# A row softmax on one core: pieces of columns for the first and the last tile, and a quarter of the scaling on another engine

## The chip, the cores and the metric

The kernel runs on one core of a Trainium2 chip. The time is device microseconds (us) of that core. The engines that matter here are VectorE (DVE in the profile), ScalarE (ACT), SyncE (SP, which does nothing but wait and issue transfers) and the core's 16 DMA engines, which move data between the chip's main memory and the on-chip memory of 128 partitions.

## The reference

A softmax over the last axis of a float32 array of 16 x 256 rows with 32768 columns, after a division by a temperature that is 1.0:

```python
scaled = logits / temperature
scaled = scaled - scaled.max(axis=-1, keepdims=True)
exp_scaled = np.exp(scaled)
return (exp_scaled / exp_scaled.sum(axis=-1, keepdims=True)).astype(np.float32)
```

Input and output are 536.87 MB each.

## The kernel before

Each row of 32768 columns is laid over two neighbouring partitions, as two halves of 16384 columns (64 KB each). A tile is 64 rows, so 128 partitions by 16384 columns, 8.4 MB; there are 64 tiles, numbered 0 to 63. The on-chip memory holds three such tiles, in three buffers `b` = 0, 1, 2 of one tensor `xs`; tile g lives in buffer g mod 3.

A tile is loaded and stored by two DMAs of 4.2 MB. One carries the even partitions, one the odd ones (h = 0, 1, lines 79 to 89). Each partition's 64 KB are contiguous in main memory. Semaphores `ld[b][h]` and `st[b][h]` count the landings.

A tile is computed in K = 4 pieces of 4096 columns, by two engines that signal each other:

- DVE waits for both halves of the load (line 105), then reduces each piece to the negated maximum of each partition (line 107).
- ACT takes each piece as its maximum arrives and replaces it with exp(x - maximum of the piece), summing as it goes (line 153).
- After the fourth exponential (line 116) DVE exchanges maxima and sums between neighbouring partitions (line 118), takes the row's maximum (line 122); ACT computes the correction of each piece, exp(piece's maximum - row's maximum), into `ee` (line 163); DVE sums the corrected sums (line 126) and takes the reciprocal (line 137).
- DVE multiplies each of the four pieces in place with its correction and the reciprocal (line 141). The last of them raises the semaphore `sc` (line 144).
- `stores` waits for `sc` and issues the two DMAs out (lines 171 to 174).

The order is written out by hand in four instruction streams. SP issues the loads of tiles 0, 1, 2 at once (183 to 185), then in a loop of 20 turns over three buffers waits for each half's store and issues the load of the next tile in its place (186 to 190), and in the end the load of tile 63 (191 to 193). DVE and ACT run the same tiles in the same order: 20 turns of three tiles, then tiles 60 to 63 written out (196 to 211). ACT issues the stores of tiles 0 to 60 itself, behind each tile's last small exponential (207, 211). SP issues the stores of tiles 61, 62 and 63, behind its last load (214 and 215), and waits for all stores (216 to 218).

## Time and profile before

| | us |
|---|---|
| median of 3 timed runs | 2526.8 |
| the runs | 2759.95, 2513.87, 2526.8 |
| profiled execution, its own time | 2492.2 |
| its span | 2490.4 |
| DVE busy | 1756.9 (71%) |
| ACT busy | 1017.9 (41%) |
| one reduce of a piece (128x4096), DVE, line 107 | 4.41 |
| one exponential of a piece, ACT, line 153 | 3.71, and 0.19 for reading the sum |
| one scaling of a piece, DVE, line 141 | 2.41 |
| first reduce begins / first store is issued | 23.4 / 55.5 |
| last reduce of tile 63 begins / its store is issued | 2449.2 / 2468.2 |

The profile is of one execution on the chip. Its page gives the busy time of each engine, the share of time in which the DMA engines were busy and the rate that they reached in 40 slices of the span, and groups of instructions by the line of the kernel. Queries of the same trace give waits, a timeline and the rates in chosen stretches. The share of the DMA engines can come out above 1 in a short stretch, since a packet is counted where it starts; stretches of a few us are read with that in mind. The profiled execution is somewhat shorter than the timed ones, so its rows are summed against its own time.

### The profile page before, as it was taken

What the parts mean: (1) busy time and instruction counts of PE and PEld (TensorE: products, weight loads), DVE (VectorE), ACT (ScalarE), POOL (GpSimd) and SP (SyncE); (2) the same over time, 40 slices, a digit from 0 to 9 for tenths busy, and PEclk for the clock granted to TensorE, in tenths of its full rate; (3) what the DMA queues carried; (4) which work ended last, traced back from release to release, by engine and by line L of the source; (5) the groups of instructions that cost most, each with busy time, mean ns of one, the idle gap of its engine ahead of it and who ended that gap; (6) DMA issues with size and microseconds to landing.
All of it is one profiled execution on the core that took longest, in us unless ns stands there. A gap on an engine that the chain in (4) does not pass through costs nothing.

```text
span 2490.4 us, 2598 instructions
## 1 busy us (share of the span) xinstructions
DVE 1756.9 (71%) x896; ACT 1017.9 (41%) x596; POOL 0.2 (0%) x4
## 2 busy tenths in 40 slices
DVE  5876676777767767777677776777767767777675
ACT  3444342534434334344353443434434335244342
POOL 0000000000000000000000000000000000000000
DMA  9999999999999999999999999999999999999999
GB/s 415 427 438 436 426 429 434 435 435 431 434 436 437 433 432 435 437 435 429 435 436 437 429 435 435 435 435 432 435 435 436 429 436 434 437 434 432 434 398 389
DMA packets 20482, 1073.77 MB, mean 431 GB/s; under 512 B 4096, under 2 KB 4096, under 8 KB 4096
## 3 DMA queue, kind: packets, MB, share of 16 engines
q1 hardware_dynamic: 10720, 562.05, 52.3%
q10 hardware_dynamic: 9760, 511.71, 47.4%
q14 instruction: 2, 0.02, 0.0%
HBM read 536.87 MB, written 536.87 MB: 431 GB/s over the span
## 4 chain that ended last, share of the span: by engine, by line
DMA 53%; DVE 24%; another core or an unknown queue 14%; ACT 4%; issue 3%; SPq 1%; DVEq 0%; ACTq 0%
DMA out_dram<-xs 29%; DMA xs<-in_logits_dram 24%; DVE t L107 17%; DVE xs L141 7%; ACT xs L153 4%; SPq L86 1%; ACT ee L163 0%; DVE t L118 0%; DVE row L137 0%; DVE row L122 0%; DVE junk L126 0%; ACTq L89 0%; DVEq L196 0%; DVEq L117 0%
## 5 line engine op out<-in xcount | busy, mean ns | idle before, releaser
L153 ACT ACTIVATE xs<-xs,t 128x4096 f32<-128x4096 f32 x256 | 949.2, 3708 | 1184.0 <-DVE t L107 1184.0
L107 DVE TENSOR_REDUCE t<-xs 128x1 f32<-128x4096 f32 x256 | 1113.4, 4411 | 425.0 <-DMA xs<-in_logits_dram 425.0
L141 DVE TENSOR_SCALAR xs<-xs,ee,row 128x4096 f32<-128x4096 f32 x256 | 600.4, 2408 | 2.3
L118 DVE LOAD_MASK_SELECT t<-t x64 | 0.9, 14 | 255.2 <-ACT xs L153 255.2
L153 ACT ACT_TABLE_LOAD x20 | 25.7, 1283 | 219.8 <-issue 218.8
L153 ACT ACTIVATION_READ_ACCUMULATOR xs<-xs,t 128x1 f32 x256 | 47.7, 186 | 0.0
L163 ACT ACTIVATE ee<-t,row 128x8 f32<-128x8 f32 x64 | 19.2, 301 | 36.7 <-DVE row L122 36.7
L126 DVE CUSTOM_DVE_ANT_1 junk<-ee,t 128x8 f32<-128x8 f32 x64 | 10.7, 167 | 23.5 <-ACT ee L163 23.5
L137 DVE RECIPROCAL row<-row 128x1 f32<-128x1 f32 x64 | 10.5, 164 | 2.2
L122 DVE TENSOR_REDUCE row<-t 128x1 f32<-128x8 f32 x64 | 10.3, 161 | 2.4 <-DVE t L118 0.3
L118 DVE STREAM_SHUFFLE t<-t 128x8 f32<-128x8 f32 x64 | 10.6, 165 | 0.6
L126 DVE DVE_READ_ACCUMULATOR2_ANT row<- 128x1 f32 x64 | 5.3, 82 | 0.0
L235 POOL MEMSET const-bfloat16-1.0<- 128x1 bf16 x1 | 0.1, 101 | 0.0
L235 POOL MEMSET const-uint8-127<- 128x1 uint8 x1 | 0.1, 101 | 0.0
L235 POOL MEMSET const-float32-0.0<- 128x1 f32 x1 | 0.1, 98 | 0.2 <-issue 0.2
L235 POOL MEMSET const-float32-1.0<- 128x1 f32 x1 | 0.1, 98 | 0.0
## 6 DMA issues: line engine op xcount, KB each, us to landing
xs<-in_logits_dram SPq DMA_DIRECT2D x128, 28.9
out_dram<-xs ACTq DMA_DIRECT2D x122, 39.8
out_dram<-xs SPq DMA_DIRECT2D x6, 24.2
```

The costliest lines, as they stand in the source:

```text
L86: sp.dma_start(out=sbuf(b, h), in_=dram(x, g, h)).then_inc(ld[b][h], 16)
L107: m = dve.tensor_reduce(out=t[:, k : k + 1], in_=self.piece(k), axis=X_, op=A.max, negate=True)
L118: dve.stream_shuffle(out=t[:, 2 * K : 4 * K], in_=t[:, 0 : 2 * K], mask=swap).then_inc(site(tag, "sh"), 1)
L122: dve.tensor_reduce(out=r[:, 0:1], in_=tv[:, :, 0, :], axis=XY, op=A.min).then_inc(site(tag, "mx"), 1)
L126: dve.tensor_tensor_reduce(out=j[:, 0 : 2 * K].rearrange("p (a k) -> p a k", a=2), in0=e[:, 0 : 2 * K].rearrange("p (a k) -> p a k", a=2), ...
L137: dve.reciprocal(out=r[:, 2:3], in_=r[:, 1:2]).then_inc(site(tag, "rc"), 1)
L141: s = dve.tensor_scalar(out=xs, in0=xs, scalar1=e[:, k : k + 1], scalar2=r[:, 2:3], op0=A.mult, op1=A.mult)
L153: a = act.activation(out=xs, in_=xs, func=Exp, bias=t[:, k : k + 1], scale=inv_t, accum_out=t[:, K + k : K + k + 1],)
L163: act.activation(out=e[:, 0 : 2 * K].rearrange("p (a k) -> p a k", a=2), in_=tv[:, :, 0, :], func=Exp, bias=r[:, 0:1], scale=-1.0,).then_i ...
L235: nc = _bacc.Bacc("TRN2", target_bir_lowering=False, num_devices=1)
```

## The change

Three edits:

- Tile 0 is loaded by four DMAs, one for each piece of 4096 columns over all 128 partitions (16 KB of each partition), with a semaphore each, `pieces[k]`. DVE waits for piece k just ahead of its reduce. To this end tile 0 is taken out of the loops of DVE and ACT: `first()` is tile 0, the loops hold tiles 1 to 60, and tiles 61 to 63 are written out behind them. SP's loops are unchanged.
- In every tile DVE scales three pieces. It also multiplies the last piece's correction with the reciprocal into one factor per partition, `r[:, 3:4]`, and ACT multiplies the last piece with that factor, by an activation with the function Copy and the factor as its scale. Each scaling raises a semaphore of its own, `sc` with k. `stores` waits for those of pieces 2 and 3 (DVE works in order, so piece 2 stands for 0 and 1).
- Tile 63 is stored by four DMAs, one for each piece of columns, each issued by SP when that piece is scaled.

```diff
+    def columns(b, k):
+        return X[:, b * _W + k * _STEP : b * _W + (k + 1) * _STEP]
+
+    def dram_columns(t, g, k):
+        return t[bass.ds(g * P, P), k * _STEP : (k + 1) * _STEP]
...
-            for h in range(_PARTS):
-                dve.wait_ge(ld[self.b][h], self.landed)
             for k in range(K):
+                for sem, value in self.landed if k == 0 or self.fine else []:
+                    dve.wait_ge(sem[k] if self.fine else sem, value)
...
-            for k in range(K):
+            dve.tensor_tensor(
+                out=r[:, 3:4], in0=e[:, K - 1 : K], in1=r[:, 2:3], op=A.mult
+            ).then_inc(site(tag, "f"), 1)
+            for k in range(K - 1):
                 xs = self.piece(k)
-                s = dve.tensor_scalar(
+                dve.tensor_scalar(
                     out=xs, in0=xs, scalar1=e[:, k : k + 1], scalar2=r[:, 2:3], op0=A.mult, op1=A.mult
-                )
-            s.then_inc(site(tag, "sc"), 1)
+                ).then_inc(site(tag, "sc", k), 1)
...
+            xs = self.piece(K - 1)
+            act.wait_ge(site(tag, "f"), n)
+            act.activation(out=xs, in_=xs, func=Copy, scale=r[:, 3:4]).then_inc(
+                site(tag, "sc", K - 1), 1
+            )

         def stores(self, q, g):
-            q.wait_ge(site(self.tag, "sc"), self.n)
+            for k in range(K - 2, K):
+                q.wait_ge(site(self.tag, "sc", k), self.n)
             for h in range(_PARTS):
                 store(q, g, self.b, h)
...
+        def stores_in_columns(self, q, g, sem):
+            for k in range(K):
+                q.wait_ge(site(self.tag, "sc", k), self.n)
+                q.dma_start(out=dram_columns(o, g, k), in_=columns(self.b, k)).then_inc(sem, 16)
...
+    pieces = [nc.alloc_semaphore(f"piece{k}") for k in range(K)]
+    for k in range(K):
+        sp.dma_start(out=columns(0, k), in_=dram_columns(x, 0, k)).then_inc(pieces[k], 16)
+    for b in range(1, _BUFS):
         for h in range(_PARTS):
             load(b, b, h)
...
+    first().vector()
     with dve.Fori(1, turns + 1) as i:
-        for b in range(_BUFS):
-            turn(b, i).vector()
-    for g in range(G - 4, G):
+        for q in range(_BUFS):
+            turn(q, i).vector()
+    for g in range(G - 3, G):
         last(g).vector()
...
+    first().scalar()
+    first().stores(act, 0)
     with act.Fori(1, turns + 1) as i:
-        for b in range(_BUFS):
-            tile_ = turn(b, i)
+        for q in range(_BUFS):
+            tile_ = turn(q, i)
             tile_.scalar()
-            tile_.stores(act, i * _BUFS + (b - _BUFS))
-    for g in range(G - 4, G):
+            tile_.stores(act, i * _BUFS + (q + 1 - _BUFS))
+    for g in range(G - 3, G):
         last(g).scalar()
...
+    end = nc.alloc_semaphore("end")
+    for g in range(G - 3, G - 1):
         last(g).stores(sp, g)
+    last(G - 1).stores_in_columns(sp, G - 1, end)
     for b in range(_BUFS):
         for h in range(_PARTS):
-            sp.wait_ge(st[b][h], 16 * len(range(b, G, _BUFS)))
+            sp.wait_ge(st[b][h], 16 * len(range(b, G - 1, _BUFS)))
+    sp.wait_ge(end, 16 * K)
```

More of the change, by code (lines that the diff above doesn't have):

```diff
@@ L37 @@
     Exp = mybir.ActivationFunctionType.Exp
+    Copy = mybir.ActivationFunctionType.Copy
     A = mybir.AluOpType
@@ L89, in store, with __init__ @@
         q.dma_start(out=dram(o, g, h), in_=sbuf(b, h)).then_inc(st[b][h], 16)
+    def columns(b, k):
+        return X[:, b * _W + k * _STEP : b * _W + (k + 1) * _STEP]
+    def dram_columns(t, g, k):
+        return t[bass.ds(g * P, P), k * _STEP : (k + 1) * _STEP]
     class Tile:
-        def __init__(self, tag, b, landed, n):
-            self.tag, self.b, self.landed, self.n = tag, b, landed, n
+        def __init__(self, tag, b, landed, n, fine=False):
+            self.tag, self.b, self.landed, self.n, self.fine = tag, b, landed, n, fine
         def piece(self, k):
-            return X[:, self.b * _W + k * _STEP : self.b * _W + (k + 1) * _STEP]
+            return columns(self.b, k)
         def vector(self):
@@ L169, in scalar, with first, turn @@
             ).then_inc(site(tag, "ee"), 1)
+            xs = self.piece(K - 1)
[3 more added lines that the diff above has]
+            )
         def stores(self, q, g):
-            q.wait_ge(site(self.tag, "sc"), self.n)
+            for k in range(K - 2, K):
+                q.wait_ge(site(self.tag, "sc", k), self.n)
             for h in range(_PARTS):
                 store(q, g, self.b, h)
-    def turn(b, i):
-        return Tile(f"q{b}", b, i * 16, i)
-    def last(g):
-        return Tile(f"l{g}", g % _BUFS, (g // _BUFS + 1) * 16, 1)
-    for b in range(_BUFS):
+        def stores_in_columns(self, q, g, sem):
+            for k in range(K):
+                q.wait_ge(site(self.tag, "sc", k), self.n)
+                q.dma_start(out=dram_columns(o, g, k), in_=columns(self.b, k)).then_inc(sem, 16)
+    def first():
+        return Tile("f", 0, [(pieces, 16)], 1, fine=True)
+    def turn(q, i):
+        b = (q + 1) % _BUFS
+        return Tile(f"q{q}", b, [(ld[b][h], i * 16) for h in range(_PARTS)], i)
+    def last(g):
+        b = g % _BUFS
+        n = len(range(b, g + 1, _BUFS)) - (b == 0)
+        return Tile(f"l{g}", b, [(ld[b][h], n * 16) for h in range(_PARTS)], 1)
+    pieces = [nc.alloc_semaphore(f"piece{k}") for k in range(K)]
+    for k in range(K):
+        sp.dma_start(out=columns(0, k), in_=dram_columns(x, 0, k)).then_inc(pieces[k], 16)
+    for b in range(1, _BUFS):
         for h in range(_PARTS):
@@ L193 @@
         load(G - 1, 0, h)
+    first().vector()
     with dve.Fori(1, turns + 1) as i:
-        for b in range(_BUFS):
-            turn(b, i).vector()
-    for g in range(G - 4, G):
+        for q in range(_BUFS):
+            turn(q, i).vector()
+    for g in range(G - 3, G):
         last(g).vector()
+    first().scalar()
+    first().stores(act, 0)
     with act.Fori(1, turns + 1) as i:
-        for b in range(_BUFS):
-            tile_ = turn(b, i)
+        for q in range(_BUFS):
+            tile_ = turn(q, i)
             tile_.scalar()
-            tile_.stores(act, i * _BUFS + (b - _BUFS))
-    for g in range(G - 4, G):
+            tile_.stores(act, i * _BUFS + (q + 1 - _BUFS))
+    for g in range(G - 3, G):
         last(g).scalar()
-        if g == G - 4:
-            last(g).stores(act, g)
-    for g in range(G - 3, G):
+    end = nc.alloc_semaphore("end")
+    for g in range(G - 3, G - 1):
         last(g).stores(sp, g)
+    last(G - 1).stores_in_columns(sp, G - 1, end)
     for b in range(_BUFS):
         for h in range(_PARTS):
-            sp.wait_ge(st[b][h], 16 * len(range(b, G, _BUFS)))
+            sp.wait_ge(st[b][h], 16 * len(range(b, G - 1, _BUFS)))
+    sp.wait_ge(end, 16 * K)
 _INS = ['logits', 'temperature']
```

## The prediction

> **What bounds the kernel now.** I read the page's table of engine busy time first, then its DMA row, then the DMA rates in stretches of the span, and only then the waits. The busy table and the 40 slices say which engine could be the limit:

> ```profile
> span 2490.4 us, 2598 instructions
> DVE 1756.9 (71%) x896; ACT 1017.9 (41%) x596; POOL 0.2 (0%) x4
> ...
> DMA  9999999999999999999999999999999999999999
> GB/s 415 427 438 436 426 429 434 435 435 431 434 436 437 433 432 435 437 435 429 435 436 437 429 435 435 435 435 432 435 435 436 429 436 434 437 434 432 434 398 389
> DMA packets 20482, 1073.77 MB, mean 431 GB/s; under 512 B 4096, under 2 KB 4096, under 8 KB 4096
> ```

> Neither compute engine is near full, and the transfer engines are over 90% busy in every slice. The reader should see that the rate sits at 434 to 437 in most slices and falls in the first and the last two only. 1073.74 MB is the input read once and the output written once; no version of this kernel moves less. At 434 GB/s that is 2474 us of the span of 2490.4. So everything that could be gained without a faster transfer is about 16 us, 0.7%.

> Where those 16 us are is shown by the same rates, in stretches that I cut at the places where they change. Columns are the stretch, its length, busy time of DVE, ACT and POOL, the clock, the mean busy share of the transfer engines, and GB/s:

> ```profile
> 0.00:2.40 2.40, 0.00 (x0) 1.28 (x1) 0.20 (x4) 1.00 0.50 164
> 2.40:60.00 57.60, 32.14 (x16) 15.82 (x10) 0.00 (x0) 1.00 1.02 430
> 60.00:120.00 60.00, 51.06 (x28) 30.69 (x18) 0.00 (x0) 1.00 0.97 419
> ...
> 500.00:1000.00 500.00, 354.51 (x182) 206.68 (x121) 0.00 (x0) 1.00 1.00 434
> 1000.00:1500.00 500.00, 354.50 (x182) 206.69 (x121) 0.00 (x0) 1.00 1.00 434
> ...
> 2410.00:2415.00 5.00, 5.00 (x2) 4.47 (x3) 0.00 (x0) 1.00 0.15 66
> 2415.00:2465.00 50.00, 41.06 (x25) 25.40 (x16) 0.00 (x0) 1.00 1.00 419
> 2465.00:2469.00 4.00, 3.17 (x2) 0.00 (x0) 0.00 (x0) 1.00 0.08 33
> 2469.00:2489.00 20.00, 0.00 (x0) 0.00 (x0) 0.00 (x0) 1.00 0.97 419
> 2489.00:2490.40 1.40, 0.00 (x0) 0.00 (x0) 0.00 (x0) 1.00 0.00 0
> ```

> Missing bytes divided by 434 give lost time: 5.0 x (1 - 66/434) = 4.2 us at 2410, 4.0 x (1 - 33/434) = 3.7 us at 2465, 1.5 us before the first byte, 1.4 us after the last, 2.6 us in all between 2.4 and 120, some 2.4 between 2415 and 2489 outside the hole at 2465. Between 120 and 2404 nothing is missing, though DVE and ACT idle there for hundreds of us. That is the ring of three buffers working as it should, with a transfer always outstanding. **A compute step made shorter there buys nothing.**

> The transfer queue's own waits on SP (waiter, releaser, us in total, times, longest) and the end of the DVE timeline (start, length, instruction) say what the holes are:

> ```profile
> SPq L86 <- DMA out_dram<-xs: 2325.7, 122, 67.8
> SPq L89 <- DVE xs L141: 51.2, 2, 30.5
> ```

> ```profile
> 2458.59 0.17 DVE L137 RECIPROCAL row<-row 128x1 f32<-128x1 f32 x1
> 2458.79 9.38 DVE L141 TENSOR_SCALAR xs<-xs,ee,row 128x4096 f32<-128x4096 f32 x4
> ```

> The hole at 2410 belongs to SP: tile 63's second half of a load waits for a store of tile 60, and the store of tile 61, whose data DVE finished near 2397.7, stands behind that load in SP's queue. The hole at 2465 belongs to DVE: everything older has been written out, and the store of tile 63 is issued only when all four of its scalings are done, at 2468.2.

> **The first tile in four column pieces.** Two issues become four on SP. An issue takes SP 0.47 to 0.64 us by its group, so the first six, from 0.96 on, are out by 4.8 and eight by 6.1, while the queued 25 MB last until about 60 us. That costs nothing. DVE can reduce piece 0 once 2.1 MB have come, 2.4 + 2.1 MB / 434 = 7.2 us and a little, instead of 23.4. The last piece lands near 23 as before. Then one reduce (4.4), one exponential (3.7 + 0.2), the small steps (1.2 by the timeline, and the new product 0.2) and three scalings (7.0) end near 40, against 55.2. The store is issued 15 us sooner. But the stretch 2.4 to 60 already runs at 430 GB/s on loads alone: the early store only shares engines that were full, and tiles 1 and 2 land later by what it takes. What is late next is the load of tile 2, still the transfers. Value: 0. This term could be a gain of at most the 2.6 us missing before 120.

> **A quarter of the scaling on ScalarE.** It removes one of four DVE scalings (9.38 / 4 = 2.35 us per tile) and adds a 128x1 product on DVE. No such row exists; the nearest are RECIPROCAL 128x1 at 0.164 and the accumulator read at 0.082 below, the 128x8 ACTIVATE at 0.301 above. I take 0.17, and 0.03 for the wait ahead of it: a net gain of 2.15 us of DVE per tile. ACT gains a Copy on 128x4096. Lower bound DVE's scaling of that shape, 2.41; upper bound the exponential at 3.71 with a table load (1.28) on each side, 6.3; I take 3.7, the same shape on the same engine. ACT then works 1017.9 + 64 x 3.7 = 1255 us, half the span. Behind the waiting Copy stand the issues of this tile's stores and the next tile's exponentials; the former need DVE's third scaling anyway (7.0 us after the product, longer than 3.7, or 6.3 with both loads), the latter need DVE's next reduce. So neither is later than today. In the 62 inner tiles all of this lies beside full transfers: 0 us either way, and the cover stays until a tile's computation grows by several us (DVE still waits 425.0 us over 60 tiles for loads, 7 us each).

> [...]

> **The tail.** Tile 62: DVE's scaling starts 0.2 later than 2426.95 and ends after 7.0, at 2434.2 instead of 2436.3. Tile 63's load has landed by then or little later: its second half was issued at 2413.9, the shortest load takes 12.7 from issue to landing, so 2426.6 at the earliest, and DVE found it there at 2436.3 without a wait. So DVE reduces from 2434.2 to 2451.6; the last exponential ends at 2455.5, the small steps at 2456.9. Pieces are scaled at 2459.2, 2461.6 and 2463.9 by DVE, and piece 3 by ACT at 2460.8. Each store can be issued then, by 0.5 to 0.8 us of SP time each. The older stores keep the transfers fed until 2465. Piece 0 is there 6 us before that (4 if the load landed as late as 2436), and each piece holds 2.1 MB / 434 = 4.8 us of work, so the queue no longer runs dry: the hole of 3.7 us closes. The 20 us of writing and the 1.4 us of ending stay.

> The hole at 2410 stays too: SP's order of load 63 ahead of store 61 is unchanged, and both wait on transfers, not on compute.

> **Column transfers.** The old halves move rows of 64 KB, the new pieces 128 rows of 16 KB; no row shows those. Below: 434 GB/s, the best of any long stretch, so no gain. Above, if every one of the eight pieces paid its start alone: the shortest time from issue to landing of a 4.2 MB half is 11.4 us, of which the bytes need 9.7, so 1.7 each, 14 us. I take 0.2 in all, because queued halves show no such price (430 GB/s over the first six). [...]

> **Sum.** 0 - 3.7 + 0.2 = -3.5 us on a span of 2490.4: 2486.9, and with the 1.8 us around it 2488.7 in place of 2492.2, a ratio of 0.9986. The profiled run is faster than all three timed ones (2513.9, 2526.8, 2760.0), so the kernel itself scatters by more than the effect. On the median of 2526.8 the ratio gives 2523.

> **Rivals.**
> 1. *Nothing arrives* (15%): the hole moves, because a late transfer makes tile 63 land after 2440 and every later us of landing shifts the pieces. 2490 to 2494 profiled, 2525 to 2529 on the median. For it: an inferior rate of 419 in 2415 to 2465 shows that the stretch is not perfectly packed. Against: 4 to 6 us of margin at piece 0.
> 2. *Column pieces are slow* (15%, the other side, slower): the place is tile 0's load and tile 63's store, 16.8 MB, 38.7 us at 434. At half rate they take 38.7 more: 2527 profiled, 2562 on the median. It decides from 3.7 / 8 = 0.46 us per piece, a rate under 397 GB/s. The 14 us bound gives 2502 and 2537. For it: no row shows 16 KB rows. Against: no short transfer in the first 60 us pays anything visible.
> 3. *The holes all close* (8%): the earlier ring start also shifts the phase of loads and stores so that 2410 is covered and the early 2.6 us come back: 2492.2 - 10.5 = 2482, on the median 2516.
> 4. *The scaling isn't split*, as where each Copy brings table loads: still hidden, as reckoned above; time of the forecast.

> Forecast, rival 4 within it: 62%. A change over 2% needs 50 us; gains end at 16, and rival 2 needs 0.42 of the rate or less: faster 0.03, same 0.92, slower 0.05; 2% is also about what a measurement of this kernel can tell from no change. The range must hold both kinds of run: its lower end is the profiled run with rival 3's gain (2482, rounded up to 2484), the upper the median with the 14 us bound and some of rival 2 (2545).

> **What would show it.** In the changed profile: no stretch under 300 GB/s after 2450, the first store at about 40 us with the rate up to 60 us unchanged, DVE busy near 1756.9 - 64 x (2.41 - 0.17) = 1614, ACT near 1255, the hole near 2410 still there, 20 table loads. Wrong would be a rate under 400 in the first 20 or last 20 us, or a span that falls by more than 12.

## The result and the profile after

The change made the kernel slower by a fifth: 3068.5 us median (2961.4 to 3133.9, 8 runs) against 2520.3 (2491.9 to 2837.1, 8 runs) of the kernel before. The ratio is 1.191, with a 95% interval of 1.173 to 1.209. The forecast was 2523 with a range of 2484 to 2545. Both kernels scatter from execution to execution; the ratios in this document compare each kernel's executions near its fastest.

The page of the profiled execution after the change (2961.4 us, span 2959.7), its busy table, the rates in 40 slices and two of its instruction groups:

```profile
span 2959.7 us, 2709 instructions
DVE 1613.3 (55%) x896; ACT 1230.9 (42%) x641; POOL 0.2 (0%) x4
...
DMA  9999999999999999898999999999999999999988
GB/s 394 346 346 339 346 345 343 346 347 353 337 353 342 353 337 349 329 368 353 383 391 370 380 384 368 384 382 369 372 381 373 380 370 370 393 370 380 384 326 373
DMA packets 21314, 1073.77 MB, mean 363 GB/s; under 512 B 4160, under 2 KB 4160, under 8 KB 4160
...
L181 ACT ACTIVATE xs<-xs,row 128x4096 f32<-128x4096 f32 x64 | 237.4, 3710 | 40.5 <-DVE row L146 40.5
...
L146 DVE TENSOR_TENSOR row<-ee,row 128x1 f32<-128x1 f32 x64 | 10.2, 159 | 2.2
```

The compute side is as reckoned: DVE 1613 us busy, the Copy 3.71 us, the product 0.16. The bytes are the same too. The transfer engines are as busy as before, at 9 tenths and more nearly everywhere, and yet move some 330 to 390 GB/s in place of 434. **A busy share does not show this loss; only the rate does.** The packets themselves take longer: a load or store of one 64 KB row took 2.42 us on its engine before, and here, between 100 and 500 us, loads average 3.0 and stores 2.7 (from the trace's packet records).

Stretches of the same execution, with the columns of the prediction's table (length, busy DVE, ACT, POOL, clock, share of the transfer engines, GB/s), show when it begins:

```profile
2.40:40.00 37.60, 25.49 (x14) 19.21 (x10) 0.00 (x0) 1.00 1.02 440
40.00:66.00 26.00, 19.21 (x12) 16.43 (x10) 0.00 (x0) 1.00 0.99 363
66.00:120.00 54.00, 30.10 (x17) 21.99 (x11) 0.00 (x0) 1.00 0.96 351
120.00:500.00 380.00, 192.40 (x103) 143.84 (x75) 0.00 (x0) 1.00 0.95 344
```

The column pieces of tile 0 load at 440 GB/s, without any price. The rate falls at 40 us, and the first store is issued at 39.6. It never comes back to 434. What the trace records of landings gives the first hint. A half lands in sixteen parts, as many as the core has DMA engines (4096 landings for the 256 halves before); the moments here are those of the first part to land. The half load that runs beside the first half store (tile 2's and tile 0's) lands at 63.2 and the store at 63.4: they end together. In the profile before, the first load and store half that run side by side land at 64.9 and 72.1.

### The profile page after: what moved, and what is told of

Same layout as the page of the kernel before. It is cut to its first block, busy times and chain, and to the rows that moved or that the text cites. A ratio compares the mean times of both kernels' runs of the same rounds, so it can differ in the third digit from the quotient of the medians.

```text
span 2959.7 us, 2709 instructions
## 1 busy us (share of the span) xinstructions
DVE 1613.3 (55%) x896; ACT 1230.9 (42%) x641; POOL 0.2 (0%) x4
## 2 busy tenths in 40 slices
DMA packets 21314, 1073.77 MB, mean 363 GB/s; under 512 B 4160, under 2 KB 4160, under 8 KB 4160
## 4 chain that ended last, share of the span: by engine, by line
DMA 59%; DVE 20%; another core or an unknown queue 16%; ACT 3%; SPq 1%; issue 0%; ACTq 0%; DVEq 0%
DMA xs<-in_logits_dram 32%; DMA out_dram<-xs 27%; DVE t L114 14%; DVE xs L151 5%; ACT xs L162 3%; SPq L87 0%; ACT ee L172 0%; DVE t L125 0%; DVE row L144 0%; DVE row L129 0%; DVE junk L133 0%; DVE row L146 0%; ACTq L90 0%; SPq L212 0%
## 5 line engine op out<-in xcount | busy, mean ns | idle before, releaser
L151 DVE TENSOR_SCALAR xs<-xs,ee,row 128x4096 f32<-128x4096 f32 x192 | 451.4, 2407 | 0.0
L181 ACT ACTIVATE xs<-xs,row 128x4096 f32<-128x4096 f32 x64 | 237.4, 3710 | 40.5 <-DVE row L146 40.5
L144 DVE RECIPROCAL row<-row 128x1 f32<-128x1 f32 x64 | 10.5, 163 | 2.2
L146 DVE TENSOR_TENSOR row<-ee,row 128x1 f32<-128x1 f32 x64 | 10.2, 159 | 2.2
## 6 DMA issues: line engine op xcount, KB each, us to landing
xs<-in_logits_dram SPq DMA_DIRECT2D x126, 45.1
```

What stands on the lines that cost most here:

```text
L144: dve.reciprocal(out=r[:, 2:3], in_=r[:, 1:2]).then_inc(site(tag, "rc"), 1)
L146: dve.tensor_tensor(out=r[:, 3:4], in0=e[:, K - 1 : K], in1=r[:, 2:3], op=A.mult).then_inc(site(tag, "f"), 1)
L151: dve.tensor_scalar(out=xs, in0=xs, scalar1=e[:, k : k + 1], scalar2=r[:, 2:3], op0=A.mult, op1=A.mult).then_inc(site(tag, "sc", k), 1)
L181: act.activation(out=xs, in_=xs, func=Copy, scale=r[:, 3:4]).then_inc(site(tag, "sc", K - 1), 1)
```

## The experiments

### One edit at a time, and a late first store

Three kernels have one edit each. The fourth is the whole change with the first store held back:

```diff
     first().scalar()
+    for h in range(_PARTS):
+        act.wait_ge(ld[2][h], 16)
     first().stores(act, 0)
```

The first edit alone:

> Only the first of the three edits: tile 0 loaded in four column pieces; DVE scales all four pieces, tile 63 is stored in two halves as before. Phase theory (the early first store, at 40 us, meets loads still queued, and from then on loads and stores keep step packet by packet, which slows every packet): the first store is issued at about 42, the rate falls to about 345 from there, time 2950 to 3130. ScalarE theory (the Copy on ScalarE, by its traffic to the on-chip memory, slows the transfers): 2490 to 2525.

The second alone:

> Only the second edit: ScalarE scales a quarter of each tile; tile 0 is loaded and tile 63 stored in two halves as before. Phase theory: the first store is issued at about 53, nearly as late as before, so packets stay at 2.4 us and the time is 2485 to 2525. ScalarE theory: the rate is 345 to 380 through the span, time 2950 to 3130.

The third alone:

> Only the third edit: tile 63 stored in four column pieces, everything else as before. Both theories: steady state as before, the hole before the last store all but closes (first piece scaled 7 us earlier, at 2461 in the span of before), 2488 to 2522, ratio 0.998.

The whole change with the late store:

> The whole change, with one wait more: ScalarE issues the first store only when both halves of tile 2 have landed, near 60 us, so that no load is queued when the first store starts. Phase theory: the ring starts as before, packets at 2.4 us, time 2485 to 2525. ScalarE theory, or a theory by which the column pieces or the loop's new order slow it: 2950 to 3130.

| kernel | first store issued, us | time, us (4 runs each, 8 of the whole change) |
|---|---|---|
| first edit alone | 41.9 | 2490.1 (2489.6 to 2490.8) |
| second edit alone | 53.1 | 2498.5 (2493.2 to 2506.7) |
| third edit alone | 55.3 | 2499.4 (2491.3 to 2511.5) |
| whole change, late store | 61.6 | 2500.8 (2495.3 to 2506.0) |
| whole change | 39.6 | 3068.5 (2961.4 to 3133.9) |

No edit is slow by itself, and the whole change is not slow either once its first store comes later. So neither ScalarE's Copy nor the column pieces slow the transfers by themselves. But the phase theory as I had written it fell too. By it the first edit alone had to be slow, since its first store at 41.9 also meets queued loads of tile 2; it ran in 2490. Between 39.6 and 41.9 something sharper decides. At 41.8 tile 1's second half lands and tile 2's first begins. The landings (again of the first part) tell the two cases apart: with the first edit alone the load half lands at 59.3 and the store half at 64.1, 4.8 us apart, which is one 64 KB row of each stream at 2.42 us. In the changed kernel it is 0.2 us. Load and store halves have the same rows in the same order in the code; with landings 0.2 us apart I took it that the same rows of a tile are written and read there side by side.

### The moment of the first store, and nothing else

The new theory: two streams that touch the same rows side by side slow each other, and one row of distance is enough. Two kernels change the moment by some 2.4 us, in opposite ways. One is the whole change with a wait that costs 2.5 us:

```diff
     first().scalar()
+    act.wait_ge(ld[1][1], 16)
     first().stores(act, 0)
```

> The whole change, with one wait more: ScalarE issues the first store only when both halves of tile 1 have landed, 42 us, some 2.5 us later than without; two halves of tile 2 are still queued then. Row theory (a load and a store of the same rows of a tile, written and read by the engines side by side, slow each other; the first store's moment decides how many rows of 64 KB the two streams stand apart, and 39.6 us makes it none): the store's rows then run one row behind the load's as in the run of the first edit alone, packets at 2.4 us, 2485 to 2505. Theory that ScalarE's scaling together with column pieces, or an early ring as such, slows it: 2950 to 3130.

The other is the first edit alone, made 2.4 us earlier by letting ScalarE scale a quarter of one tile in 64:

```diff
-            for k in range(K):
+            if self.fine:
+                dve.tensor_tensor(
+                    out=r[:, 3:4], in0=e[:, K - 1 : K], in1=r[:, 2:3], op=A.mult
+                ).then_inc(site(tag, "f"), 1)
+            for k in range(K - self.fine):
...
+            if self.fine:
+                xs = self.piece(K - 1)
+                act.wait_ge(site(tag, "f"), n)
+                act.activation(out=xs, in_=xs, func=Copy, scale=r[:, 3:4]).then_inc(
```

> The first edit alone, and ScalarE scales a quarter of tile 0 only; tiles 1 to 63 are scaled by DVE alone and tile 63 is stored in halves. This does nothing but bring the first store from 41.9 to 39.6 us. Row theory: no row apart, 345 GB/s from 40 us on, 2900 to 3130. Theory that ScalarE's work in the inner tiles matters: 2488 to 2495, as with the first edit alone.

The whole change with the small wait took **2486.8 us** (2486.3 to 2487.1, 4 runs; ratio to the kernel before 0.996, 0.993 to 0.999). The first edit with one Copy more took **3062.5** (3015.8 to 3086.4; ratio 1.214, 1.198 to 1.230). The same stretches, first of the whole change with the wait:

```profile
40.00:66.00 26.00, 19.32 (x12) 16.55 (x10) 0.00 (x0) 1.00 0.97 403
66.00:120.00 54.00, 32.61 (x18) 21.87 (x11) 0.00 (x0) 1.00 1.03 444
120.00:500.00 380.00, 250.57 (x140) 192.14 (x100) 0.00 (x0) 1.00 1.00 433
```

and of the first edit with the one Copy:

```profile
40.00:66.00 26.00, 19.31 (x11) 15.51 (x9) 0.00 (x0) 1.00 0.99 368
66.00:120.00 54.00, 32.08 (x17) 15.51 (x9) 0.00 (x0) 1.00 0.95 347
120.00:500.00 380.00, 211.76 (x104) 119.02 (x68) 0.00 (x0) 1.00 0.95 345
```

and of the first edit alone, for comparison:

```profile
40.00:66.00 26.00, 21.06 (x12) 15.51 (x9) 0.00 (x0) 1.00 0.96 403
66.00:120.00 54.00, 37.66 (x19) 15.51 (x9) 0.00 (x0) 1.00 1.03 445
120.00:500.00 380.00, 271.04 (x140) 155.04 (x90) 0.00 (x0) 1.00 1.00 433
```

First stores at 42.1, 39.5 and 41.9 us; 433, 345 and 433 GB/s for hundreds of us after. The first edit alone and the first edit with the one Copy do the same work in 63 of 64 tiles and take 2490 and 3062 us, by the moment of one store.

The landings show that the distance is handed on from tile to tile. Sort the sixteen parts of a store by time, and those of the load beside it, and compare them one by one: in the changed kernel all sixteen of the store land 0.2 us after those of the load, at every pair up to 681 us; with the small wait they land 4.8 to 9.0 us after, at every pair up to 2400 us. The order of the code fits that: each load is issued when a store lands, and it queues behind another half (a load of the changed kernel lands 45.1 us after its issue in the median, against 28.9 before), so row follows row.

### What must be shared: the probe

Is it the rows in main memory, the partitions on the chip, or the turning between reading and writing? A kernel without the softmax runs stages of four loads and, from the same moment, four stores:

```diff
+        for c in range(4):
+            b, h = 1 + c // 2, c % 2
+            sp.dma_start(out=half(b, h), in_=rows(x, (out_tile + 2 + c // 2) * P + h)).then_inc(ls, 16)
+            if part is not None:
+                act.dma_start(
+                    out=rows(o, (out_tile + c // 2) * P + row(h)), in_=half(0, part(h))
+                ).then_inc(ss, 16)
```

> No softmax: after a load of tile 0, eight stages, each of four loads of halves on SP's queue and at the same moment four stores of halves on ScalarE's queue, from tile 0's buffer; every stage waits for all. The output is not filled. Stage 1 loads alone; 2 and 8 store the same parity of partitions to the same rows of a tile as the load beside them; 3 the other parity of both; 4 the same partitions, rows of the other parity in main memory; 5 the other partitions, the same rows in main memory; 6 and 7 the same partitions, rows 2 and 8 further in main memory. Row theory, main memory: 2, 5 and 8 at 345 GB/s (97 us), the rest at 430 (77 us), 7 open. Row theory, on-chip partitions: 2, 4, 6, 7 and 8 slow, 3 and 5 fast. If turning between loads and stores in step is the cause: 2 to 8 all slow. If none is slow, the slow packets need something that the probe lacks.

Its eight stages as stretches (POOL is the only engine with instructions; the last column is GB/s, the start and the end of a stage included):

```profile
23.30:64.90 41.60, 0.00 (x0) 1.00 0.95 403
64.90:165.60 100.70, 0.00 (x0) 1.00 0.91 333
165.60:248.00 82.40, 0.00 (x0) 1.00 0.96 407
248.00:348.60 100.60, 0.00 (x0) 1.00 0.91 334
348.60:431.10 82.50, 0.00 (x0) 1.00 0.96 407
431.10:530.50 99.40, 0.00 (x0) 1.00 0.91 338
530.50:630.80 100.30, 0.00 (x0) 1.00 0.91 335
630.80:732.70 101.90, 0.00 (x0) 1.00 0.90 329
```

Stages 3 and 5 take 82 us, all other mixed stages 99 to 102. In 3 and 5 the store reads the partitions of the other parity. Where it writes them in main memory changes nothing: the same rows (stage 5, 82.5 us) are fast, rows of the other parity, or 2 or 8 rows on (4, 6, 7, 99.4 to 100.6 us), are slow. So it is **the on-chip partitions**: a transfer that reads a partition beside one that writes it. The buffers differ; their columns lie 64 or 128 KB apart in each partition, and that does not help. Other distances of columns were not tried. Turning between directions is not it: then stages 3 and 5, with the same four loads beside four stores, had to be slow too.

A second probe put one row of distance into the same partitions, by a store of one row for each engine ahead of the others, and tried shifts:

> No softmax; stages as in the first probe (four loads beside four stores, all waited for), the output not filled. 1: 64 partitions, the store from the load's partitions in the same order: slow, 345 GB/s. 2: the same, but one row (64 KB on each engine) of other partitions is stored first, so that every store runs one row behind the load beside it: 430 by the row theory. 3 to 7 take 56 partitions: 3 same, slow; 4 the store stands 2 partitions (one row of the same engine) further: 430; 5 and 6 it stands 8 and 16 partitions further, so that a partition is read by one engine while the next one or the one after writes it in step: slow if the partition is what two streams may not share, fast if it is one engine's reading and writing of one partition; 7 other parity: 430. 8: four column pieces of 16 KB rows over 128 partitions, in step on the same partitions: 345 if it is a matter of partitions alone, nearer 430 if the short rows drift apart.

```profile
23.20:123.60 100.40, 0.00 (x0) 1.00 0.91 334
123.60:209.20 85.60, 0.00 (x0) 1.00 0.96 404
```

Same partitions in step take 100.4 us; one row behind they take 85.6, with 1.05 MB more to move. That is about the distance of the changed kernel with the small wait, shown without a softmax around it. Stages 3 to 7, with 56 partitions, ran at 249 to 271 GB/s whatever the shift, the other parity included: something else limited DMAs of that shape, and nothing follows. The share of the transfer engines was 0.79 to 0.84 in them, and 0.91 and 0.96 in stages 1 and 2. That fits 14 of the 16 engines with four rows each, since 14/16 of 0.91 to 0.96 is 0.80 to 0.84: an estimate from these shares, for no record says which engine moves which row. The column pieces in step (stage 8) took 48.1 us for 16.8 MB. With the 5 us of start and end that stage 3 of the first probe shows beyond its bytes (82.4 against 77.3), 434 GB/s would give 44 and 345 would give 54, so by this estimate short rows in step lose some, but less than half as much.

> No softmax; stages of four loads beside four stores, all waited for, the output not filled. Each DMA has 32 partitions of one parity, two rows of 64 KB for each of 16 engines, since 56 partitions had not run on all engines. The store stands further than the load by: stage 1, 0 partitions; 2, 2 (the engine's other row); 3, 4 (the next engine's rows); 4, 8; 5, 32; 6, 64; 7, the other parity; 8, 0 again. 16.8 MB a stage: 39 us and some 4 of start and end at 434 GB/s, some 10 us more at 345. If one partition's reading and writing in step by the same engine is what is slow: only 1 and 8. If reading and writing in step anywhere in the same parity (whichever engine, whichever partition) is slow: 1 to 6 and 8. [...]

All eight stages took 60 to 62 us, 271 to 281 GB/s, again with the other parity as slow as the rest. All the loads lay in the first 64 partitions; stage 6, whose stores lay in the other 64, took 60 us too. What limited these DMAs stays open, and nothing follows for the cause. Whether the reading and the writing must be on the same DMA engine stays open.

### The other parity in the kernel

The last test of the theory in the kernel itself leaves every moment alone and changes which partitions meet:

```diff
+    def order(b):
+        return (1, 0) if b == 1 else (0, 1)
...
-            for h in range(_PARTS):
+            for h in order(self.b):
                 store(q, g, self.b, h)
...
-            for h in range(_PARTS):
+            for h in order(b):
                 sp.wait_ge(st[b][h], i * 16)
+                if b == 1:
+                    sp.sem_inc(site("seen"), 1)
```

The initial loads follow the same order. `seen` is a counter that nobody waits for.

> The whole change, except that buffer 1 is loaded and stored odd partitions first, then even ones; buffers 0 and 2 keep their order. In the early ring the load of tile g+2 runs beside the store of tile g, so two of three pairs now meet with opposite parity and one in step. Row theory: a third of the loss is left, 2490 + (3060 - 2490) / 3 = 2680, within 2560 and 2780; packets slow in every third pair. If the loss comes from the early store or the ring as such, or if which partitions meet makes no difference: 2950 to 3130.

It took 2728.1 us (2719.1 to 2732.0; ratio 1.092, 1.084 to 1.100), inside the expected range. Stretches cut at the landings, first one pair of tiles in step, then two pairs of opposite parity, then the same again:

```profile
43.00:86.00 43.00, 24.42 (x14) 19.21 (x10) 0.00 (x0) 1.00 0.97 366
86.00:164.50 78.50, 50.41 (x28) 38.43 (x20) 0.00 (x0) 1.00 1.00 427
164.50:209.60 45.10, 25.21 (x14) 19.21 (x10) 0.00 (x0) 1.00 0.96 355
209.60:288.00 78.40, 50.41 (x28) 38.43 (x20) 0.00 (x0) 1.00 0.99 425
```

One tile in 43 to 45 us, then two in 78.4, which is 39.2 each: the slow third is where the theory puts it. Over the whole run more than a third of the loss is left (241 of 582 us, against the run with the small wait); what makes up the rest was not looked for.

### Without ScalarE's quarter

> The first and the third edit, with the first store held until both halves of tile 1 have landed; DVE scales all four pieces. Against the run of the whole change with that wait (2486.8) it lacks ScalarE's quarter alone. If the quarter is worth nothing beside full transfers: 2486 to 2489. If it is needed to close the hole before the last store: 2489 to 2492.

2487.0 us (2484.9 to 2491.9, 10 runs; ratio to before 0.996, 0.993 to 0.998) against 2486.8 with the quarter: it is worth nothing beside full transfers. These two are the fastest kernels here, 0.4% under the kernel before.

## Why the prediction was wrong

**What bounds the kernel: right, with a wrong constant.** The transfers do bound it, and compute beside them is worth nothing. The step that failed is the term of the first tile, "Value: 0", with its reason, "the early store only shares engines that were full": it takes 434 GB/s for the price of a byte whatever runs beside it. I had read 434 in every long stretch and taken it for a property of the engines. Here it also depends on how far the store stands from the load beside it: 434 GB/s with a row between them, 344 in step. Priced at 0, the early store measured 474 us between two profiled executions (2959.7 against 2485.4) that differ in one wait at the start. The slices of the profile before also dip to 426 and 429 in mid-run, and not in the first and last two alone, as I wrote; nothing rests on that.

**The moved store.** I counted its 15 us as harmless because the transfers were busy. The prediction gave the right moment (near 40; it was 39.6) and never asked what would stand beside the store then: tile 2's halves, row for row, in place of the last rows of the initial loads.

**The rivals.** None of them was it. The third did say that an earlier start shifts the phase of loads and stores, but as a gain of 10.5 us. The column pieces were the right object to doubt, for the wrong reason: their own rate was 440 GB/s. My bound for them, 1.7 us a piece, covered the transfers that were new and left out the 252 old ones whose neighbours they changed. Tile 0's queued pieces showed no such price: the last of the four began to land at 22.5 us, the second half before at 22.7.

**ScalarE's quarter: right in its prices, wrong in tile 0.** DVE 1613 us against 1614 predicted, the Copy 3.71 against 3.7, the product 0.16 against 0.17. ACT came to 1231 and not 1255, since table loads fell from 20 (25.7 us) to 1 (1.3 us), where I had expected the 20 of the page before; the 64 Copies brought none. Beside full transfers none of it moved the time (2486.8 us with the quarter, 2487.0 without). But in tile 0 it brought the first store from 41.9 to 39.5 us, and that alone took the first edit from 2490 to 3062 us. The two edits that I had priced at 0 each were harmful only together.

**The tail: right in its mechanism, too large in its size.** The third edit alone closes the hole at 2465. Its stretches:

```profile
2465.00:2469.00 4.00, 2.90 (x2) 0.00 (x0) 0.00 (x0) 1.00 0.95 406
2469.00:2484.00 15.00, 0.00 (x0) 0.00 (x0) 0.00 (x0) 1.00 1.01 434
2484.00:2488.10 4.10, 0.00 (x0) 0.00 (x0) 0.00 (x0) 1.00 0.22 92
```

406 GB/s where there were 33. But the span only fell from 2490.4 to 2489.5, 0.9 us for the 3.7 in my sum. The last line says where the rest went: parts that lag behind the others used to catch up in the hole, and now the end waits for them, 4.1 us at 92 GB/s. In the profile before, the parts of the last half ahead of the hole land from 2465.6 to 2468.9, and those of the last store within 0.2 us; with the third edit the parts of the last store land within 3.6 us. The whole change with the small wait has a span of 2485.4, 5.0 under the profile before; the hole at 2410, which I had expected to stay, is mostly gone from it too:

```profile
2410.00:2415.00 5.00, 5.00 (x2) 4.47 (x3) 0.00 (x0) 1.00 0.88 380
2415.00:2420.00 5.00, 5.00 (x2) 4.47 (x4) 0.00 (x0) 1.00 0.94 301
```

So the sum of -3.5 us would have been near for a change whose first store came 2.5 us later, but by luck: the first edit alone shortens the span by 2.2 us (to 2488.2), where the sum had 0, and the third alone by 0.9, where it had 3.7.

## What to carry to other kernels

When transfers bound a kernel, ask of any moved transfer what it will run beside, not only whether the engines are free; a full busy share can hide a fifth of the rate (here 0.95 at 344 GB/s, and 1.00 at 433 with the small wait), so read GB/s and the time of a packet. The ring of buffers here handed the distance between loads and stores on from tile to tile (0.2 us at every pair up to 681 us), and one store issued 2.4 us earlier took the run from 2490 to 3062 us. Where loads and stores share the partitions row for row, as here, keep them at least one row apart; here a wait on a load that was already due did it (2486.8 us in place of 3068.5).
